# Stick-breaking attention: sums over later key blocks taken on VectorE ahead of the product with ones

## The chip, the cores and the metric

The kernel runs on one core of one Trainium2 chip. The metric is the device time of one execution in microseconds. TensorE (PE) multiplies matrices, VectorE (DVE), ScalarE (ACT) and GpSimd (POOL) work on tiles, SyncE (SP) issues most DMAs. Tiles lie in SBUF, products in PSUM, which has eight banks of 128 x 512 numbers.

## The reference

Two layers of a streaming encoder over 512 frames with 1024 features. Each layer has a token mixer with three groups of heads (retention, stick-breaking attention, gated linear attention), which share one input projection and one output projection, and then a feed-forward part with a short convolution. What the change touches is the stick-breaking group, six heads a layer:

```python
def stick_breaking(q, k, v):
    for blk in range(s // SB_BLOCK):            # blocks of 128 queries
        z = einsum('bhtd,bhsd->bhts', q[block], k[:end]) * d ** -0.5
        strict = s_idx < t_idx
        log_keep = where(strict, log_sigmoid(-z), 0.0)
        between = cumsum(log_keep, reverse=True) - log_keep
        a = where(strict, exp(log_sigmoid(z) + between), 0.0)
        outs.append(einsum('bhts,bhse->bhte', a, v[:end]))
```

For a query t and a key s, the weight is the sigmoid of z(t,s) times the product of 1 - sigmoid over all keys between s and t. In logarithms that is a sum over the later keys.

## The kernel before

The scores are held with keys on the partitions and queries along the columns. Key block i (128 keys) meets the queries from block i on, so it is 512 - 128 i columns wide. `REG` gives the place of each block: block 0 in PSUM tile 0 (512 columns), block 1 in tile 1 (columns 0 to 383), block 2 in tile 2 (256 columns), block 3 in tile 1 (columns 384 to 511). A "part" below is one of these PSUM tiles.

With L = softplus(z) (masked), the exponent that is wanted is z minus the sum of L over the same and later keys up to the query. `sb_head` makes it in three steps. First the scores and the mask go into the three PSUM tiles. Then, part by part in the order 2, 1, 0, ScalarE takes |z|, exp and ln (L780, and twice the helper at L226), VectorE adds max(z, 0) (L783), and the result L is split in two halves of the fast matmul format: ScalarE casts the high half (L785), VectorE subtracts it from L for the low half (L786). Last, TensorE adds -L to the scores: for block i the product of a triangle of -1 (`tri`) with block i's own L, and one product of a matrix of -1 (`negones`) with the L of each later block, each for the high and the low half: ten pairs, 20 products. Then ScalarE takes the exponential of each part, and `weigh` multiplies with the values.

The mixer is written as generators that are pumped in the order of a string of tokens: g for the linear attention, s for stick-breaking and retention in turn, p for a step of the input projection, f for a step of the conditioning vectors (VectorE reductions over `ada` tiles, L255). The program's scheduler then orders each engine's instructions from this; each engine takes its own in that order. So projection products (tiles `pj`) stand between the products of a head. All matmuls are issued at the recorder's line L92. Tiles of 128 x 512 (`T`, names `m__...`) share one pool of 52 buffers, and the scores of all chains share five PSUM banks (`ps`). Weights come by DMA as `raw`, and are split into `hi` (L361, ScalarE) and `lo` (L362, VectorE).

Of the kernel before, what the change touches and what calls it, by code (L numbers as in the profile page):

```python
# [12 lines left out]
F32R = mybir.dt.float32r  # L13
# [3 lines left out]
ALU = mybir.AluOpType  # L17
AX = mybir.AxisListType

P = 128  # L20
# [78 lines left out]
def trunk(ctx: ExitStack, tc: tile.TileContext, A, out, dbg=None):  # L99
# [18 lines left out]
    def nm(s):  # L118
        cnt[0] += 1
        return f"{s}_{cnt[0]}"  # L120

    def T(tag="m", shape=(P, 512), dt=F32):
        tag = TMAP.get(tag, tag)
        return tiles[tag].tile(list(shape), dt, tag=tag, name=nm(tag + "_"))
# [11 lines left out]
    def psz():  # L136
        return bank("pz")
# [7 lines left out]
    V, SC, G, PE = nc.vector, nc.scalar, nc.gpsimd, Recorder(nc.tensor)  # L145

    @contextmanager
    def seq(kind):

        mode = MODE[kind]  # L150
        m = (None, PE.last, PE.lastp)[mode]
        if m is not None:
            with tc.issue_after(m.ins):
                yield
        else:
            yield
        if kind == "p":
            PE.lastp = PE.last

    lastw = [None]  # L160
    start = {"on": True, "ld": None, "pe": None, "ws": []}
# [21 lines left out]
    def as32(t):  # L183
        return t.bitcast(F32)
# [39 lines left out]
    def act(*a, **k):  # L224
        with tc.issue_after(tables[0].ins):
            last_act[0] = SC.activation(*a, **k)  # L226
# [150 lines left out]
    REG = ((0, 0, 512), (1, 0, 384), (2, 0, 256), (1, 384, 128))  # L377
# [24 lines left out]
    def scores(par, qs, ql, ks):  # L402
        ps = [psz() for _ in range(3)]
        for i, (b, o, w) in enumerate(REG):
            kc, qc = slice(i * P, i * P + P), slice(i * P, S)
            PE.matmul(ps[b][:, o : o + w], ks[par][:, kc], qs[par][:, qc], start=(i < 3), stop=False, skip_group_check=True)
            PE.matmul(ps[b][:, o : o + w], ks[par][:, kc], ql[par][:, qc], start=False, stop=True, skip_group_check=True)
        return ps
# [38 lines left out]
    C = {}  # L447
# [95 lines left out]
    def mixer(l, hnh, hnl, after):  # L543
# [225 lines left out]
        def sb_head(par, qs, ql, ks, at):  # L769
            with seq("s"):  # L770
                ps = scores(par, qs, ql, ks)
                for i, (b, o, w) in enumerate(REG):
                    PE.matmul(ps[b][:, o : o + P], C["identb"], C["negm"], start=False, stop=True,
                              skip_group_check=True)
            Lh, Ll = [None] * 3, [None] * 3
            for b in (2, 1, 0):
                w = WID[b]
                z = ps[b][:, :w]
                e = T()
                SC.activation(e[:, :w], z, AF.Abs)  # L780
                act(e[:, :w], e[:, :w], AF.Exp, scale=-1.0)
                act(e[:, :w], e[:, :w], AF.Ln, bias=onec, scale=1.0)
                V.scalar_tensor_tensor(e[:, :w], z, 0.0, e[:, :w], ALU.max, ALU.add)  # L783
                Lh[b], Ll[b] = T("hl", dt=F32R), T("hl", dt=F32R)
                SC.copy(Lh[b][:, :w], e[:, :w])  # L785
                V.tensor_tensor(Ll[b][:, :w], e[:, :w], as32(Lh[b][:, :w]), ALU.subtract)  # L786
                at[par][b] = e
            yield
            with seq("s"):
                for i in (3, 2, 1, 0):  # L790
                    b, o, w = REG[i]
                    for i2 in range(i, 4):
                        b2, o2, w2 = REG[i2]
                        m = C["tri"] if i2 == i else C["negones"]
                        d = (i2 - i) * P
                        for X in (Lh, Ll):
                            PE.matmul(ps[b][:, o + d : o + w], m, X[b2][:, o2 : o2 + w2], start=False, stop=True,
                                      skip_group_check=True)
            for b in (2, 1, 0):
                act(at[par][b][:, : WID[b]], ps[b][:, : WID[b]], AF.Exp)  # L800
            yield

        def sb_pair(j):
            (qs, ql), ks = need(f"sq{j}", f"sk{j}")
            at = [[None] * 3, [None] * 3]
            for par in range(2):
                yield from sb_head(par, qs, ql, ks, at)
            need("sv")
            with seq("s"):
                o = weigh(at, sv, P * j)  # L810
            mh[3 + j], ml[3 + j] = split(o)
            tap(f"sb{l}{j}", as32(mh[3 + j]))
            yield
# [76 lines left out]
        for tb in range(NTB):  # L890
            cs = slice(tb * P, tb * P + P)
            ps = psz()
# [76 lines left out]
    if WARM:  # L969

        ps = psz()
# [21 lines left out]
    b2 = pv[0][:, PV["sh1"] : PV["sh1"] + 2 * KT].rearrange("p (n k) -> p n k", n=2)  # L993
# [174 lines left out]
```

## Time and profile before

| | us |
|---|---|
| median of 3 runs (1389.92 to 1395.08) | 1392.14 |
| the profiled execution | 1393.45 |
| its span, first to last instruction | 1391.7 |
| TensorE busy | 1354.5 (97%) |
| VectorE busy | 838.3 (60%) |
| ScalarE busy | 633.3 (46%) |
| GpSimd busy | 54.0 (4%) |

The profile is one execution. An engine's busy time is the union of its instructions. Matmuls overlap and their ends are modelled, so the distance from one start to the next says what a matmul costs in a row of them. The heads of layer 0 lie between 95 and 275 us, those of layer 1 between 780 and 980 us.

### The profile page before, as it was taken

The numbers are of one execution on the slowest core, as the hardware profiler recorded it, in microseconds if no ns is written. First come the engines' busy times: TensorE is split into PE (matmuls) and PEld (weight loads), VectorE is DVE, ScalarE is ACT, GpSimd is POOL, SyncE is SP. The second block draws the span as 40 slices with busy tenths as digits, with TensorE's granted clock in tenths as the row PEclk, the third lists the DMA queues.
The fourth block names the chain that finished last, engine by engine and source line by source line (L and its number), as shares of the span: only waits on it lengthen the run. The fifth ranks groups of instructions, "written<-read, shape, count | busy, mean of one in ns | idle before, by whom it ended". The sixth has DMA issues, their size and how long they took to land.

```text
span 1391.7 us, 19758 instructions
## 1 busy us (share of the span) xinstructions
PE 1354.5 (97%) x7619; PEld 1110.6 (80%) x7619; DVE 838.3 (60%) x1572; ACT 633.3 (46%) x1033; POOL 54.0 (4%) x97
## 2 busy tenths in 40 slices
PE   8999999999999999999999999999999999999997
PEld 5887667767988888888899877777898888888886
DVE  4559988665888874424563587776565444443232
ACT  5455465765543333322254556675564333332220
POOL 1000000001000000000020000000010000000000
PEclk9999999999999999999999999999999999999999
DMA  9635461204677852233753222111343223222233
GB/s 323 222 119 170 156 210 59 77 32 165 233 254 254 260 187 100 91 105 119 241 172 123 69 92 76 46 62 61 122 151 113 99 92 106 91 98 100 91 106 106
DMA packets 73999, 186.22 MB, mean 134 GB/s; under 512 B 8833, under 2 KB 9905, under 8 KB 73905
## 3 DMA queue, kind: packets, MB, share of 16 engines
q1 hardware_dynamic: 72512, 182.68, 38.9%
q0 software_dynamic: 1088, 2.12, 0.4%
q8 instruction: 60, 0.98, 0.3%
q14 instruction: 35, 0.28, 0.1%
q10 hardware_dynamic: 304, 0.16, 0.1%
HBM read 176.51 MB, written 8.41 MB: 133 GB/s over the span
## 4 chain that ended last, share of the span: by engine, by line
PE 65%; DVE 5%; ACT 3%; DMA 1%; issue 1%; POOL 0%; DVEq 0%; POOLq 0%; SPq 0%; ACTq 0%
PE pj L92 40%; PE ps L92 25%; DVE lo L362 1%; ACT hi L361 1%; DMA m__707_3526<-x 0%; DMA m__1755_9280<-x 0%; DMA raw<-wu 0%; DMA raw<-wT 0%; ACT junk L516 0%; ACT junk L307 0%; POOL s L295 0%; DVE hnl L342 0%; ACT m__1632_8684 L226 0%; DVE m__1675_8921 L742 0%; DVE m__1460_7779 L742 0%
## 5 line engine op out<-in xcount | busy, mean ns | idle before, releaser
L362 DVE TENSOR_TENSOR lo<-raw,hi 128x1024 fp32r<-128x1024 f32 (+2 forms) x208 | 245.7, 1183 | 258.2 <-ACT hi L361 250.0
L92 PE MATMUL pj<-hnh,lo 128*128 128x512 f32 x976 | 382.3, 392 | 2.0 <-DVE lo L362 2.0
L92 PE MATMUL pj<-hnh,hi 128*128 128x512 f32 x976 | 383.6, 393 | 0.0
L92 PE MATMUL pj<-hnl,hi 128*128 128x512 f32 x976 | 382.1, 392 | 0.0
L361 ACT CAST hi<-raw 128x1024 fp32r<-128x1024 f32 (+2 forms) x208 | 211.5, 1018 | 334.9 <-PE pj L92 171.0
L92 PEld LDWEIGHTS pj<-hnh,lo 128*128 128x128 f32 x976 | 183.7, 188 | 40.5 <-DVE lo L362 2.3
L92 PEld LDWEIGHTS pj<-hnh,hi 128*128 128x128 f32 x976 | 183.7, 188 | 39.7 <-issue 2.8
L92 PEld LDWEIGHTS pj<-hnl,hi 128*128 128x128 f32 x976 | 183.6, 188 | 37.7 <-issue 0.8
L255 DVE SCALAR_TENSOR_TENSOR ada<-ada,cB 128x512 f32<-128x512 f32 x160 | 107.2, 686 | 32.1 <-DMA ada<-ada 31.1
L92 PE MATMUL pj<-hi,hnh 128*128 128x384 f32 (+1 forms) x160 | 51.2, 320 | 0.0
L92 PE MATMUL pj<-lo,hnh 128*128 128x384 f32 (+1 forms) x160 | 50.9, 318 | 0.0
L92 PE MATMUL pj<-hi,hnl 128*128 128x384 f32 (+1 forms) x160 | 50.9, 318 | 0.0
L295 POOL TENSOR_TENSOR s<-s,nhalf 128x1 f32<-128x1 f32 x32 | 20.4, 638 | 760.0 <-DVE s L293 756.4
L92 PE MATMUL ps<-hnl,hi 128*128 128x256 f32 x128 | 36.4, 288 | 1.1 <-DVE hnl L342 1.1
L92 PE MATMUL ps<-hnh,lo 128*128 128x256 f32 x128 | 35.8, 284 | 0.0
L92 PE MATMUL ps<-hnh,hi 128*128 128x256 f32 x128 | 35.8, 289 | 0.0
L524 ACT ACTIVATE junk<-ps 128x512 bf16<-128x512 f32 x16 | 9.6, 597 | 51.5 <-PE ps L92 51.3
L92 PEld LDWEIGHTS pj<-hi,hnh 128*128 128x128 f32 x160 | 30.1, 188 | 0.5
L92 PEld LDWEIGHTS pj<-lo,hnh 128*128 128x128 f32 x160 | 30.0, 188 | 0.3
L92 PEld LDWEIGHTS pj<-hi,hnl 128*128 128x128 f32 x160 | 30.1, 188 | 0.0
L92 PEld LDWEIGHTS ps<-hnl,hi 128*128 128x128 f32 x128 | 24.6, 193 | 1.5 <-DVE hnl L342 1.3
L92 PEld LDWEIGHTS ps<-hnh,hi 128*128 128x128 f32 x128 | 24.7, 197 | 0.0
(2786 smaller groups left out, 2485.5 us busy)
## 6 DMA issues: line engine op xcount, KB each, us to landing
raw<-wu SPq DMA_DIRECT2D x88, 512.0 KB, 3.3
ada<-ada SPq DMA_DIRECT2D x160, 256.0 KB, 3.5
raw<-wd SPq DMA_DIRECT2D x44, 512.0 KB, 3.2
raw<-wT SPq DMA_DIRECT2D x42, 512.0 KB, 3.5
raw<-wo SPq DMA_DIRECT2D x16, 512.0 KB, 3.2
raw<-wsv SPq DMA_DIRECT2D x8, 384.0 KB, 3.6
raw<-wrv SPq DMA_DIRECT2D x8, 384.0 KB, 3.1
raw<-wgv SPq DMA_DIRECT2D x8, 272.0 KB, 2.7
```

Of the source, the lines that this page charges most:

```text
L92: self.last = self.e.matmul(*a, **k)
L255: V.scalar_tensor_tensor(raw, raw, 1.0, cB[h], ALU.mult, ALU.mult, accum_out=pt[:, 4 * h + j : 4 * h + j + 1])
L295: G.tensor_tensor(r, v, nhalf, ALU.pow)
L361: SC.copy(h, raw)
L362: V.tensor_tensor(l_, raw, as32(h), ALU.subtract)
L524: SC.activation(junk, ps, AF.Square, accum_out=ss)
```

## The change

VectorE forms the sums of L over the later blocks, and each block has one product with `negones` for each half instead of one for each later block. Part 1 comes first now. The unused half of part 2's tile takes L2 (a copy on GpSimd) and L2 + L3 for the queries that have both, so that it holds what block 1 needs; a further tile s takes L1 (a copy on GpSimd) and L1 + L2 (+ L3), which block 0 needs. Both are split into halves as L is.

```diff
-            Lh, Ll = [None] * 3, [None] * 3
-            for b in (2, 1, 0):
+            Lh, Ll, E_ = [None] * 4, [None] * 4, [None] * 3
+            for b in (1, 2, 0):
                 w = WID[b]
                 z = ps[b][:, :w]
                 e = T()
...
                 V.scalar_tensor_tensor(e[:, :w], z, 0.0, e[:, :w], ALU.max, ALU.add)
+                E_[b] = at[par][b] = e
+                if b == 2:
+                    G.tensor_copy(e[:, 256:384], e[:, 0:128])
+                    V.tensor_tensor(e[:, 384:512], e[:, 128:256], E_[1][:, 384:512], ALU.add)
+                    w = 512
                 Lh[b], Ll[b] = T("hl", dt=F32R), T("hl", dt=F32R)
                 SC.copy(Lh[b][:, :w], e[:, :w])
                 V.tensor_tensor(Ll[b][:, :w], e[:, :w], as32(Lh[b][:, :w]), ALU.subtract)
-                at[par][b] = e
+                if b == 2:
+                    s = T("hl")
+                    G.tensor_copy(s[:, 0:128], E_[1][:, 0:128])
+                    V.tensor_tensor(s[:, 128:384], E_[1][:, 128:384], e[:, 256:512], ALU.add)
+                    Lh[3], Ll[3] = T("hl", dt=F32R), T("hl", dt=F32R)
+                    SC.copy(Lh[3][:, :384], s[:, :384])
+                    V.tensor_tensor(Ll[3][:, :384], s[:, :384], as32(Lh[3][:, :384]), ALU.subtract)
             yield
             with seq("s"):
                 for i in (3, 2, 1, 0):
                     b, o, w = REG[i]
-                    for i2 in range(i, 4):
-                        b2, o2, w2 = REG[i2]
-                        m = C["tri"] if i2 == i else C["negones"]
-                        d = (i2 - i) * P
-                        for X in (Lh, Ll):
-                            PE.matmul(ps[b][:, o + d : o + w], m, X[b2][:, o2 : o2 + w2], start=False, stop=True,
-                                      skip_group_check=True)
+                    for X in (Lh, Ll):
+                        PE.matmul(ps[b][:, o : o + w], C["tri"], X[b][:, o : o + w], start=False, stop=True,
+                                  skip_group_check=True)
+                    for X in (Lh, Ll) if i < 3 else ():
+                        t, c = ((X[3], 0), (X[2], 256), (X[1], 384))[i]
+                        PE.matmul(ps[b][:, o + P : o + w], C["negones"], t[:, c : c + w - P], start=False, stop=True,
+                                  skip_group_check=True)
```

In the changed file the new lines stand as follows: L787 and L795 are the copies on GpSimd, L788 and L796 the additions on VectorE, L791 and L792 the halves of a part (before L785 and L786), L798 and L799 the halves of s; Abs is L781 (before L780).

ScalarE's order in the first head, from the cast of the second part on. ps_189, ps_188 and ps_187 are parts 2, 1 and 0; an exponential that reads a ps tile into an m tile without onec is the final one. Before:

```order
L785 CAST m__194_1025<-m__193_1020 128x512
L780 ACTIVATE m__196_1029<-ps_187_996 128x512
L226 ACTIVATE m__196_1029<-m__196_1029 128x512
L226 ACTIVATE m__196_1029<-m__196_1029,onec_99 128x512
L226 ACTIVATE m__190_1011<-ps_189_998 128x256
L226 ACTIVATE m__193_1020<-ps_188_997 128x512
L785 CAST m__197_1034<-m__196_1029 128x512
```

With the change:

```order
L791 CAST m__194_1027<-m__193_1020 128x512
L798 CAST m__197_1034<-m__196_1031 128x384
L226 ACTIVATE m__193_1020<-ps_189_998 128x256
L226 ACTIVATE m__190_1011<-ps_188_997 128x512
L781 ACTIVATE m__199_1038<-ps_187_996 128x512
L226 ACTIVATE m__199_1038<-m__199_1038 128x512
L226 ACTIVATE m__199_1038<-m__199_1038,onec_99 128x512
L791 CAST m__200_1043<-m__199_1038 128x512
```

The final exponentials of parts 2 and 1 stood behind part 0's Abs, Exp and Ln, and stand ahead of them now; the cast of s (L798) has come in ahead of both. Over the twelve heads, both stand ahead of part 0's Abs in five, that of part 2 alone in four, none in three.

TensorE's order at the products into part 0 of the first head (ps_187), from the product with the low half's triangle on. Before:

```order
L92 MATMUL ps_187_996<-m__198_1035,tri_642 128x512
L92 MATMUL ps_187_996<-m__194_1025,negones_646 128x384
L92 MATMUL ps_187_996<-m__195_1026,negones_646 128x384
L92 MATMUL ps_187_996<-m__191_1016,negones_646 128x256
L92 MATMUL ps_187_996<-m__192_1017,negones_646 128x256
L92 MATMUL ps_187_996<-m__194_1025,negones_646 128x128
L92 MATMUL ps_187_996<-m__195_1026,negones_646 128x128
L92 MATMUL pj_241_1256<-lo_201_1041,hnh_3_116 128x384
```

With the change:

```order
L92 MATMUL pj_244_1259<-hi_212_1067,hnl_4_117 128x384
L92 MATMUL ps_187_996<-m__200_1043,tri_642 128x512
L92 MATMUL ps_187_996<-m__201_1044,tri_642 128x512
L92 MATMUL ps_187_996<-m__197_1034,negones_646 128x384
L92 MATMUL ps_187_996<-m__198_1035,negones_646 128x384
L92 MATMUL pj_267_1356<-hi_203_1049,hnh_3_116 128x384
```

The six products with negones are two, both over the sum tile s, and the two with the triangle stand next to each other without projection products between.

## Rows read from the trace of the kernel before

**Rows 1.** The page's head and first block: span; busy us, share, instructions.

```profile
span 1391.7 us, 19758 instructions
...
PE 1354.5 (97%) x7619; PEld 1110.6 (80%) x7619; DVE 838.3 (60%) x1572; ACT 633.3 (46%) x1033; POOL 54.0 (4%) x97
```

**Rows 2.** Stretches: length, busy PE, PEld, DVE, ACT, POOL, clock, DMA.

```profile
95.00:275.00 180.00, 170.04 (x1255) 131.22 (x1254) 153.66 (x339) 106.78 (x181) 10.24 (x19) 0.99 0.42 138
...
340.00:705.00 365.00, 361.00 (x1704) 302.87 (x1703) 234.59 (x475) 130.23 (x188) 12.62 (x22) 1.00 0.56 185
...
780.00:980.00 200.00, 193.91 (x1444) 150.93 (x1443) 146.70 (x271) 127.85 (x217) 7.51 (x13) 1.00 0.18 61
```

**Rows 3.** Timeline of TensorE, head one, block 1: start, duration, instruction.

```profile
104.19 0.22 PE L92 MATMUL ps<-m__194_1025,negones 128*128 128x128 f32 x1
...
104.36 0.39 PE L92 MATMUL pj<-hi,hnl 128*128 128x384 f32 x1
```

**Rows 4.** Timeline of TensorE, head one, block 0; idle time in brackets.

```profile
107.19 0.50 PE L92 MATMUL ps<-m__198_1035,tri 128*128 128x512 f32 x1 [0.19 <-DVE m__198_1035 L786]
...
107.88 0.28 PE L92 MATMUL ps<-m__191_1016,negones 128*128 128x256 f32 x1
...
108.12 0.22 PE L92 MATMUL ps<-m__194_1025,negones 128*128 128x128 f32 x1
...
108.29 0.39 PE L92 MATMUL pj<-lo,hnh 128*128 128x384 f32 x1
```

**Rows 5.** Timeline of ScalarE, head one.

```profile
96.09 0.39 ACT L780 ACTIVATE m__190_1011<-ps 128x256 f32<-128x256 f32 x1 [1.16 <-PE ps L92]
...
98.46 0.41 ACT L785 CAST m__191_1016<-m__190_1011 128x256 fp32r<-128x256 f32 x1 [1.00 <-DVE m__190_1011 L783]
98.77 0.59 ACT L780 ACTIVATE m__193_1020<-ps 128x512 f32<-128x512 f32 x1
...
101.55 0.62 ACT L785 CAST m__194_1025<-m__193_1020 128x512 fp32r<-128x512 f32 x1 [0.76 <-DVE m__193_1020 L783]
102.07 0.59 ACT L780 ACTIVATE m__196_1029<-ps 128x512 f32<-128x512 f32 x1
...
103.99 0.37 ACT L226 ACTIVATE m__190_1011<-ps 128x256 f32<-128x256 f32 x1
...
105.14 0.62 ACT L785 CAST m__197_1034<-m__196_1029 128x512 fp32r<-128x512 f32 x1
```

**Rows 6.** Timeline of VectorE, head one, two low halves.

```profile
99.03 0.42 DVE L786 TENSOR_TENSOR m__192_1017<-m__190_1011,m__191_1016 128x256 fp32r<-128x256 f32 x1
...
102.52 0.69 DVE L786 TENSOR_TENSOR m__195_1026<-m__193_1020,m__194_1025 128x512 fp32r<-128x512 f32 x1
```

**Rows 7.** Timeline of VectorE, a retention pair, other widths.

```profile
239.79 0.55 DVE L827 TENSOR_TENSOR m__488_2466<-ps,m__346_1789 128x384 f32<-128x384 f32 x1
...
240.59 0.28 DVE L827 TENSOR_TENSOR m__488_2466<-ps,m__346_1789 128x128 f32<-128x128 f32 x1
```

**Rows 8.** Timeline of GpSimd, 345 to 348 us.

```profile
345.45 0.55 POOL L295 TENSOR_TENSOR s<-s,nhalf 128x1 f32<-128x1 f32 x1 [5.40 <-DVE s L293]
347.32 1.57 POOL L295 TENSOR_TENSOR s<-s,nhalf 128x1 f32<-128x1 f32 x1 [1.31 <-DVE s L293]
```

**Rows 9.** Timeline of VectorE at the same time.

```profile
347.25 1.23 DVE L362 TENSOR_TENSOR lo<-raw,hi 128x1024 fp32r<-128x1024 f32 x1
```

**Rows 10.** Groups of GpSimd: busy us, mean ns of one, idle before.

```profile
L664 POOL TENSOR_TENSOR m__178_950<-m__178_950,m__179_951 128x512 f32<-128x512 f32 x1 | 1.3, 1294 | 57.4 <-ACT m__178_950 L226 57.4
...
L247 POOL MEMSET mod1g<- 128x24 f32 x2 | 0.3, 138 | 0.0
```

**Rows 11.** Timeline of TensorE, after a wait at 167 us.

```profile
169.24 0.50 PE L92 MATMUL pj<-hnh,lo 128*128 128x512 f32 x1 [2.01 <-DVE lo L362]
...
170.62 0.63 PE L92 MATMUL pj<-hnh,hi 128*128 128x512 f32 x1
171.04 0.63 PE L92 MATMUL pj<-hnl,hi 128*128 128x512 f32 x1
```

## The prediction

> **What bounds the kernel now.** I read the page's first block, then the kernel cut into stretches, then, for the stretches that the change touches, the timelines of TensorE, ScalarE and VectorE around one head, and last what TensorE waited for. The first block says TensorE: busy for 1354.5 of 1391.7 us, with VectorE at 60% and ScalarE at 46% [rows 1]. The stretches say where that holds [rows 2]. In a feed-forward part (340 to 705 us) TensorE is busy for 361.00 of 365 us. The twelve stick-breaking heads lie in 95 to 275 us (layer 0) and 780 to 980 us (layer 1). There TensorE is idle for 180 - 170.04 = 9.96 us and 200 - 193.91 = 6.09 us, together 16.05 us, while VectorE is busy 85% and 73% of the time. So TensorE bounds the heads' stretches too, but not alone: part of the time it waits for a chain that runs over ScalarE and VectorE. Within a head the reader is to see products with tri and negones that stand between projection products (pj), which fill TensorE while a head's chain runs, and a wait where the chain comes late: 0.19 us ahead of the second product of part 0 in head one [rows 4].
>
> **What is removed.** Per head the list of products with L falls from 20 to 14. Gone are, each twice (high and low half): block 3 into block 1 (128 columns), block 2 into block 0 (256) and block 3 into block 0 (128). Matmuls overlap, so a matmul's price is not its 0.22 to 0.28 us but the distance to the next start. In head one the pair into block 1 takes 104.36 - 104.19 = 0.17 us [rows 3]; the pairs into block 0 take 108.12 - 107.88 = 0.24 us and 108.29 - 108.12 = 0.17 us [rows 4]. That is 0.58 us a head and 12 x 0.58 = 7.0 us in all. The products that stay keep their widths and prices.
>
> **What is added.** On VectorE, per head: an addition over 128 columns (0.28 us, as the 128-column row of the retention scores), one over 256 columns (0.42 us), the low half of part 2 over 512 instead of 256 columns (0.69 - 0.42 = 0.27 us) and the low half of the new sum over 384 columns (0.55 us) [rows 6, 7]. Together 1.52 us, 18.2 us in twelve heads. On ScalarE: the cast of part 2 over 512 instead of 256 columns (0.62 - 0.41 = 0.21 us) and a cast over 384 (between these two, 0.52 us) [rows 5], 0.73 us a head, 8.8 us in all. Both engines have room for it (153.66 and 146.70 us busy become some 163 and 156 of 180 and 200), so these microseconds cost nothing where projection products cover them; where that cover is gone they are waits of TensorE.
>
> On GpSimd: two copies of 128 x 128 a head, which the trace of before does not show. The nearest rows bound one between 0.14 us (a memset of 24 columns) and 1.29 us (a sum of two inputs over 512 columns) [rows 10]; by columns the second makes 0.32 us, and I take 0.35 us. Each copy runs beside the VectorE addition for the same tile (0.28 and 0.42 us), so at that price it adds under 0.1 us to a head.
>
> **What is moved.** This is where the gain can go. ScalarE's queue in head one now runs 9.67 us from the first Abs (96.09) to the end of part 0's cast (105.14 + 0.62) [rows 5]. In the new order I add up the same rows: part 1 first, 102.07 - 98.77 = 3.30; part 2, 98.77 - 96.09 = 2.68, plus the addition ahead of its cast 0.28 and the wider cast 0.21, 3.17; then the cast of the new sum waits for part 2's low half and the addition on VectorE, 0.69 + 0.42 = 1.11, and takes 0.52. In head one both final exponentials now stand ahead of part 0's Abs (order shown with the change); they took 105.14 - 103.99 = 1.15 us, which used to lie in the wait for VectorE's L783. Part 0 follows: 103.99 - 102.07 = 1.92, the wait for VectorE that part 1 shows, 0.76, and the cast 0.62. Sum 12.55 us, 2.88 us more. In five of the twelve heads the order has both exponentials ahead, in four only the short one (0.37 us, so 2.10 more), in three none (1.73 more): (5 x 2.88 + 4 x 2.10 + 3 x 1.73) / 12 = 2.33 us a head in the mean, a chain 24% longer.
>
> How much of that TensorE feels, no row shows. From below it is nothing, since projections fill; even some of the 16.05 us could go, since a part's products now wait for fewer tiles. From above it is all of 12 x 2.33 = 28.0 us. I take the value nearest to what the trace shows for the chain as it is: the 16.05 us of idle time grow by the same 24%, 3.9 us. (Some of these waits belong to other chains, which makes it high; the missing slack makes it low.)
>
> **Sum.** The profiled execution took 1393.45 us, 1391.7 of span and 1.75 around it, 1.3 us above the median of the three runs, 1392.14. Against it: -7.0 + 3.9 = -3.1 us, 1390.3; against the median 1389.0. I predict 1389 us.
>
> **Rivals.**
>
> *The whole gain arrives.* Projections cover all of the longer chain, and a fifth of the idle time (3 us) goes because part 1 starts a head and its products wait for fewer halves: 1392.1 - 7.0 - 3.0 = 1382 us. For it speaks that TensorE is busy 94% and 97% of the heads' stretches, so there is work to fill with; against it that VectorE at 85% answers late.
>
> *Slower: part 0's chain is exposed.* Mechanism: ScalarE stands at the cast of the new sum, which waits for VectorE, and behind it in the same queue stand part 0's Abs, Exp and Ln, and behind these TensorE's widest products. If two thirds of the 2.33 us a head are exposed, 18.7 - 7.0 = +11.7 us, 1404 us. It decides from 0.58 us a head on (25% of the lengthening) for slower at all, from 1.17 us on for slower by 0.5%. For it: the wait of rows 4 sits at this very product. A long wait costs twice: after 2.01 us of waiting for a weight tile, TensorE's rows are spaced 171.04 - 170.62 = 0.42 us [rows 11], where the feed-forward part takes 361.00 / 1704 = 0.21 us for one in the mean [rows 2]: the lower of the two clock levels (1.2 GHz for 2.4) for a while. Against: products of other chains stand between.
>
> *The copies meet VectorE.* GpSimd's one-column power takes 0.55 us [rows 8], but 1.57 us where a VectorE subtraction of two SBUF tiles began 0.07 us earlier and ended 0.41 us before it [rows 8, 9]. If the copies lose half of that 1.02 us each, the head's chain grows by another 1.0 us to 3.3 (34%), the idle time by 5.5 us: 1390.6; if VectorE is the one held up, 24 x 0.35 = 8.4 us of the busier engine come on top, at worst in full, 1399. I put this rival at 1394 us. The Trainium skill ("SBUF — State Buffer", section "Who interferes with whom") states the rule: a VectorE instruction with two SBUF inputs contends with a GpSimd instruction that reads SBUF, not with one that only writes it. By that rule the two rows are the expected picture; GpSimd's many memsets here would be harmless, and the new copies, which read, would not.
>
> *Nothing moves.* The removed products stood where TensorE would have waited anyway, and the chain's growth is covered: 1392 us. The change itself does what it says; the order shows four products into block 0 where eight stood.
>
> **How the numbers follow.** Chances: forecast 0.43 (1389, its own range 1385 to 1396), whole gain 0.25 (1382), exposed chain 0.19 (1404), copies 0.08 (1394), nothing 0.05 (1392). What a measurement of this kernel can tell from no change is about 0.5%, 7 us: 1385 and 1399. Faster beyond that: the whole gain and a twelfth of the forecast, 0.29. Slower: the exposed chain and half of the copies, 0.23. Same: 0.48. The range leaves out a tenth at each end: 1379 to 1404.
>
> **What would show it.** Right: 72 matmuls fewer; VectorE up by about 18 us and ScalarE by about 9 us; TensorE's idle time in the heads' stretches at about 20 us; these stretches together some 3 us shorter, the feed-forward parts unchanged. The first rival shows idle time under 14 us, the exposed chain over 25 us with waits for L791, L792, L798 or L799, the copies GpSimd rows far above 0.35 us at L787 and L795. Wrong altogether would be a difference outside the heads' stretches.

## The result, and the profile after

The changed kernel takes 1425.99 us in the median (1424.88 to 1428.66) where the kernel before took 1392.31 beside it: a ratio of 1.0231 [1.0206, 1.0255]. It is 37 us above the forecast, and above the range. The page's head says how the 32.7 us between the two profiled spans divide.

```profile
span 1424.4 us, 19718 instructions
...
PE 1362.8 (96%) x7547; PEld 1107.5 (78%) x7547; DVE 855.1 (60%) x1608; ACT 638.9 (45%) x1045; POOL 62.4 (4%) x121
```

Against [rows 1]: the 72 matmuls are gone, VectorE has 16.8 us more and ScalarE 5.6, GpSimd 8.4 for its 24 copies. So the change does what it says. TensorE's idle time grew from 37.2 to 61.6 us (24.4 us), and its busy time grew by 8.3 us although it has less to do. Where, the stretches show (columns as in [rows 2]):

```profile
95.00:275.00 180.00, 161.80 (x1142) 121.26 (x1141) 151.26 (x338) 99.51 (x168) 12.53 (x25) 0.94 0.40 128
275.00:340.00 65.00, 54.60 (x311) 40.64 (x310) 38.81 (x70) 37.12 (x64) 2.69 (x6) 0.89 0.17 57
340.00:705.00 365.00, 360.22 (x1708) 302.63 (x1707) 232.19 (x464) 134.75 (x199) 10.50 (x18) 1.00 0.55 183
780.00:980.00 200.00, 191.52 (x1306) 146.04 (x1306) 142.31 (x251) 121.09 (x206) 11.74 (x25) 0.97 0.22 72
```

The feed-forward part is as before. The heads of layer 0 start where they did, but TensorE does 1142 matmuls in 180 us where it did 1255, idle for 18.2 us instead of 9.96, at a granted clock of 0.94. In the 65 us behind, where the last head of layer 0 now ends (291.4 us instead of 272.8), it is idle for 10.4 us where it was idle for 2.82. In layer 1 the heads end at 976.9 us instead of 942.5, and part of what they lose falls behind 980 us. The 65 us of before:

```profile
275.00:340.00 65.00, 62.18 (x330) 48.44 (x329) 38.04 (x77) 35.86 (x68) 2.87 (x6) 0.97 0.23 82
```

Finer stretches show where the clock falls; first three of the kernel after, then the same of before:

```profile
200.00:220.00 20.00, 14.52 (x53) 8.56 (x52) 14.49 (x28) 11.18 (x20) 2.02 (x4) 0.74 0.50 159
280.00:300.00 20.00, 10.56 (x66) 7.32 (x58) 13.08 (x22) 12.01 (x22) 2.69 (x6) 0.79 0.23 79
900.00:920.00 20.00, 15.18 (x82) 8.01 (x81) 11.61 (x19) 13.89 (x25) 2.33 (x3) 0.74 0.09 27
```

```profile
200.00:220.00 20.00, 19.57 (x92) 13.45 (x93) 15.48 (x28) 13.74 (x24) 0.00 (x0) 1.00 0.46 148
280.00:300.00 20.00, 18.46 (x130) 12.60 (x130) 11.69 (x29) 8.62 (x16) 0.00 (x0) 0.91 0.08 27
900.00:920.00 20.00, 20.00 (x158) 15.15 (x157) 18.51 (x35) 11.57 (x20) 0.00 (x0) 1.00 0.23 80
```

The longest waits of TensorE between 95 and 300 us (line and tile waited for; total, times, longest) are for the casts of the heads (L791), and one at the end of layer 0's mixer for the linear attention; the last line is the longest of layer 1, between 780 and 990 us:

```profile
PE ps L95 <- DVE m__587_2916 L709: 6.2, 1, 6.2
PE ps L92 <- ACT m__265_1352 L791: 4.0, 1, 4.0
PE ps L92 <- ACT m__380_1886 L791: 2.5, 1, 2.5
PE ps L92 <- ACT m__566_2806 L791: 2.2, 1, 2.2
PE ps L92 <- ACT m__406_2022 L791: 2.0, 1, 2.0
...
PE ps L92 <- ACT m__1535_8041 L791: 4.8, 1, 4.8
```

Added up over the whole trace, TensorE waited 2.7 us for casts of the heads in the kernel before (six waits) and 21.0 us in the changed one (15 waits). That is 18.3 of the 24.4 us of new idle time.

The second line is head two. TensorE there (start, duration, instruction, idle time and its releaser in brackets):

```profile
130.66 0.40 PE L92 MATMUL pj<-hnh,lo 128*128 128x512 f32 x1
130.99 0.69 PE L92 MATMUL ps<-m__243_1254,m__242_1253 64*64 64x64 f32 x32
132.75 1.07 PE L92 MATMUL ps<-m__199_1038,m__122_664 128*64 128x512 f32 x2 [1.07 <-ACT m__258_1329 L226]
137.79 0.76 PE L92 MATMUL ps<-m__265_1352,tri 128*128 128x512 f32 x1 [3.97 <-ACT m__265_1352 L791]
138.52 0.80 PE L92 MATMUL ps<-m__266_1353,tri 128*128 128x512 f32 x1
...
139.75 0.63 PE L92 MATMUL pj<-hnh,hi 128*128 128x512 f32 x1
140.18 0.63 PE L92 MATMUL pj<-hnl,hi 128*128 128x512 f32 x1
...
144.34 0.40 PE L92 MATMUL pj<-hnh,hi 128*128 128x512 f32 x1
144.57 0.40 PE L92 MATMUL pj<-hnl,hi 128*128 128x512 f32 x1
```

One projection product stands ahead of the gap, then 3.97 us in which TensorE stands before part 0's product; the next projection products are behind it in the queue, and none waits for anything when its turn comes. After the wait equal products start 0.43 us apart, and 0.23 us from 144.34 on: the lower of the two levels (1.2 GHz) and then the upper (2.4). The granted clock of the trace is 1.00 from 120 to 131 us, 0.72 from 137.8 to 144 and 1.00 from 144.3 to 146. What kept part 0 is in ScalarE's timeline:

```profile
128.01 0.62 ACT L791 CAST m__259_1336<-m__258_1329 128x512 fp32r<-128x512 f32 x1 [0.76 <-DVE m__258_1329 L788]
130.95 1.05 ACT L361 CAST hi<-raw 128x1024 fp32r<-128x1024 f32 x1 [2.32 <-DMA raw<-wT]
131.90 0.51 ACT L798 CAST m__262_1343<-m__261_1340 128x384 fp32r<-128x384 f32 x1
132.32 0.38 ACT L226 ACTIVATE m__258_1329<-ps 128x256 f32<-128x256 f32 x1
132.59 0.59 ACT L226 ACTIVATE m__255_1320<-ps 128x512 f32<-128x512 f32 x1
133.07 0.60 ACT L781 ACTIVATE m__264_1347<-ps 128x512 f32<-128x512 f32 x1
...
136.17 1.04 ACT L361 CAST hi<-raw 128x1024 fp32r<-128x1024 f32 x1 [1.09 <-DMA raw<-wT]
137.12 0.61 ACT L791 CAST m__265_1352<-m__264_1347 128x512 fp32r<-128x512 f32 x1
```

Part 2's cast ends at 128.63, part 0's Abs starts at 133.07. Between them stand the cast of the sum, both exponentials and a weight cast that waits 2.32 us for its DMA. A second weight cast, which waits 1.09 us, stands ahead of part 0's own cast. In the kernel before part 0's cast was through by then; its weight cast came behind it:

```profile
128.61 0.62 ACT L785 CAST m__259_1340<-m__258_1335 128x512 fp32r<-128x512 f32 x1 [0.52 <-DVE m__258_1335 L783]
131.15 1.05 ACT L361 CAST hi<-raw 128x1024 fp32r<-128x1024 f32 x1 [1.91 <-DMA raw<-wT]
```

One number sums this up, and it is used below: the *chain* of a head, from the start of its first Abs to the end of part 0's last low half (of the sum's, where that comes later). In head one it ran from 96.09 [rows 5] to 107.14 (VectorE's low half began at 106.46 and took 0.68), 11.05 us; after, from 95.77 to 109.86:

```profile
95.77 0.60 ACT L781 ACTIVATE m__190_1011<-ps 128x512 f32<-128x512 f32 x1 [1.20 <-PE ps L92]
```

```profile
109.17 0.69 DVE L792 TENSOR_TENSOR m__201_1044<-m__199_1038,m__200_1043 128x512 fp32r<-128x512 f32 x1
```

Taken so from the timelines, the mean of the twelve heads is 12.69 us before and 15.53 us after, 2.84 us more a head, 34.1 us in all.

### The profile page after: what moved, and what is told of

Read it like the earlier page. It is cut to its first block, busy times and chain, and to the rows that moved or that the text cites. A ratio compares the mean times of both kernels' runs of the same rounds, so it can differ in the third digit from the quotient of the medians.

```text
span 1424.4 us, 19718 instructions
## 1 busy us (share of the span) xinstructions
PE 1362.8 (96%) x7547; PEld 1107.5 (78%) x7547; DVE 855.1 (60%) x1608; ACT 638.9 (45%) x1045; POOL 62.4 (4%) x121
## 4 chain that ended last, share of the span: by engine, by line
PE 71%; DVE 12%; DMA 9%; ACT 5%; issue 2%; POOL 0%; SPq 0%; DVEq 0%; POOLq 0%; ACTq 0%
PE pj L92 39%; PE ps L92 32%; DMA ada<-ada 6%; DVE lo L362 3%; DVE ada L255 2%; ACT hi L361 1%; DMA raw<-wT 1%; DMA m__1820_9429<-x 0%; DMA m__117_557<-ada 0%; DVE hnl L342 0%; DMA m__725_3544<-x 0%; DMA m__7_122<-x 0%; DMA m__1247_6554<-x 0%; DMA m__1836_9506<-x 0%; DVE m__180_958 L701 0%
## 5 line engine op out<-in xcount | busy, mean ns | idle before, releaser
L255 DVE SCALAR_TENSOR_TENSOR ada<-ada,cB 128x512 f32<-128x512 f32 x160 | 106.9, 687 | 30.8 <-DMA ada<-ada 30.1
```

The source lines that it names most:

```text
L255: V.scalar_tensor_tensor(raw, raw, 1.0, cB[h], ALU.mult, ALU.mult, accum_out=pt[:, 4 * h + j : 4 * h + j + 1])
```

## The experiments

Ratios are to the kernel before, run beside each on the same chip, with 95% intervals. A chain is the mean of the twelve heads in one execution, the profiled one; a ratio comes from several executions.

### First: order, place, copies, products

**e1_order.** The kernel before, parts in the order of the change.

```diff
-            for b in (2, 1, 0):
+            for b in (1, 2, 0):
```

> The kernel before, with only the order of the parts changed from (2, 1, 0) to (1, 2, 0); no sums, the 20 products a head as before. Theory Q (ScalarE's queue: part 0's Abs stands behind the cast of the new sum, which waits for VectorE): the order alone is harmless, 1387 to 1398 us. Theory O (the order of the parts itself: with the wide part first, the final exponentials and the first products come late): most of the 34 us loss is already here, 1410 us or more. Theory C (the GpSimd copies are slow or hold up VectorE) and theory D (the added VectorE and ScalarE work lengthens the chain of a head wherever it stands): 1387 to 1398 us, as Q.

Ratio 1.000 [0.998, 1.002], chain 12.74 us. Theory O falls.

**e2_late_sum.** The block `if b == 2: s = ...` of the changed kernel, moved behind the loop over parts.

> The changed kernel, with the new sum for block 0 (copy, addition, cast, low half) made after part 0's Abs, Exp, Ln and halves instead of ahead of them; the same instructions, in another order. Theory Q: part 0 no longer waits behind the sum, at least two thirds of the 34 us come back: 1390 to 1404 us. Theory D: the same work still has to end before block 0's last products, so nothing comes back: 1420 to 1432 us. Theories O and C: 1420 to 1432 us.

Ratio 1.0263 [1.0233, 1.0293], chain 15.3 us. Theory Q falls in the form in which it was put: part 0 no longer stands behind the sum, but then the sum ends last, and the chain is as long.

**e3_copies_dve.**

```diff
-                    G.tensor_copy(e[:, 256:384], e[:, 0:128])
+                    V.tensor_copy(e[:, 256:384], e[:, 0:128])
...
-                    G.tensor_copy(s[:, 0:128], E_[1][:, 0:128])
+                    V.tensor_copy(s[:, 0:128], E_[1][:, 0:128])
```

> The changed kernel, with the two copies of 128 x 128 a head on VectorE instead of GpSimd. Theory C: without GpSimd on the path and beside VectorE, at least half of the loss comes back: 1396 to 1410 us. Theories Q, O and D: VectorE has 24 short copies more, some 0.2 us each on a busy engine, 1424 to 1434 us.

Ratio 1.0275 [1.0244, 1.0306], chain 15.86 us. Theory C falls.

**e4_sums_old_products.** The changed kernel with the loop over `i2` of the kernel before in place of the new products.

> The changed kernel with all its sums, copies, casts and order, but the 20 products a head of the kernel before (the new sums are made and not used). It separates what the added work costs from what the missing products save. If the removed products were on the path (7.0 us by their distances): 1430 to 1436 us. If TensorE would stand waiting in their place anyway: 1422 to 1429 us, as the changed kernel. If theory Q needs the products to wait for the sum itself, rather than for part 0 behind it: below 1410 us.

Ratio 1.0257 [1.0238, 1.0277], chain 16.23 us. 3.6 us more than the changed kernel, within the two intervals: the loss comes with the sums, and the missing products save little. In microseconds (1432.48) this is the first of the expected ranges, but the kernel before took 1397.54 beside it, 5 us more than with the result.

### Second: load against length

**e5_dve_load, e6_act_load.** The kernel before, with work behind the loop over parts that nothing waits for; one on VectorE, one on ScalarE.

```diff
+            V.tensor_reduce(scr[:, 0:1], at[par][1], mybir.AxisListType.X, ALU.add)
+            V.tensor_reduce(scr[:, 1:2], at[par][0], mybir.AxisListType.X, ALU.add)
```

```diff
+            SC.copy(junk[:, :256], at[par][0][:, :256])
+            SC.copy(junk[:, :128], at[par][1][:, :128])
```

> The kernel before, with two reductions over 512 columns a head added on VectorE behind part 0's low half, some 1.4 us a head, that nothing waits for: VectorE's load of the change without its longer chain. Theory V (VectorE is 96% busy between 100 and 140 us, so added work there delays all that stands behind it in its queue, above all the low halves of the weights at L362 that free the weight buffers; projections then come late and TensorE lacks them as fill): at least half of the loss appears, 1409 us or more. Theory L (the chain of the head itself got longer than the projections placed beside it can cover): nothing waits for these, 1391 to 1401 us. Theory B (three more tiles a head turn the ring of 52 buffers faster, so buffers come free late): 1391 to 1401 us.

> The kernel before, with two casts of 256 and 128 columns a head added on ScalarE behind part 0's cast, some 0.7 us a head, that nothing waits for: ScalarE's load of the change without its longer chain. Theory V: ScalarE has room, 1391 to 1400 us. Theory L: 1391 to 1400 us. At 1405 us or more ScalarE's queue would be the one that hands its delay on.

Ratios 1.0050 [1.0033, 1.0066] and 1.0015 [0.9997, 1.0033], chains 12.44 and 12.65 us. VectorE's load by itself costs 7 us, a fifth of the loss: theory V has a part, not the most.

**e7_adds_pool.** Both `V.tensor_tensor(..., ALU.add)` of the sums on GpSimd.

> The changed kernel, with the two additions a head on GpSimd as well as the copies: VectorE loses 0.28 + 0.42 = 0.70 of the 1.5 us that were added a head, and the chain of a head gets longer, since GpSimd takes 1.29 us for a sum of two inputs over 512 columns. Theory V: a third to a half of the loss comes back, 1408 to 1416 us. Theory L: slower still, 1428 us or more. Theory B: 1424 to 1432 us.

Ratio 1.0229 [1.0205, 1.0253], 1425.80 us, chain 15.0 us. Of the three ranges only that of theory B has this, and the next run speaks against B. The kernel is neither better for VectorE's sake, as V had it, nor worse for GpSimd's, as L had it; the longer chain that L counted on did not come.

**e8_nm47.** `NM` 52 to 47 in the kernel before.

> The kernel before, with 47 buffers in the ring instead of 52 (three tiles more a head on some 28 use the ring up about 10% faster). Theory B: most of the loss appears, 1410 us or more. Theories V and L: the ring has slack, 1391 to 1400 us.

Ratio 1.0035 [1.0016, 1.0054], chain 12.66 us. Five buffers are worth 5 us here, not 34: theory B falls as the main cause.

### Third: the length itself

**e9_hops.** The kernel before, with a step on GpSimd in each part.

```diff
                 V.scalar_tensor_tensor(e[:, :w], z, 0.0, e[:, :w], ALU.max, ALU.add)
+                G.tensor_copy(e[:, :256], e[:, :256])
```

> The kernel before, with one GpSimd copy of 256 columns onto itself in each of the three parts of a head, between VectorE's L783 and ScalarE's cast: no work added on TensorE, VectorE or ScalarE, only a longer chain, some 0.5 to 0.6 us a hop. Theory L in figures: from a head's first Abs to the end of its last low half the traces show 12.69 us in the mean before and 15.53 us after; 12 x 2.84 = 34.1 us is the whole loss, so every microsecond of the chain is exposed. It expects 12 x 1.6 = 19 us, 1406 to 1422 us. Theory V (VectorE's load) and theory C (GpSimd beside VectorE) expect 1391 to 1400 us.

Ratio 1.0064 [1.0042, 1.0086], chain 14.10 us. The chain grew by 1.41 us; 12 x 1.41 = 16.9 us of chain made 9 us of time, between the ranges of theories L and V. A longer chain costs. How much of it is not settled here: the chain is that of the slowest of seven executions (1408.73 us), 15.3 us above the profiled one of before, and against the median it is about half.

**e10_after_no_ln.** The changed kernel without the third step of each part.

```diff
-                act(e[:, :w], e[:, :w], AF.Ln, bias=onec, scale=1.0)
```

> The changed kernel without the logarithm of the three parts (left out: ScalarE's L783, so the sums are not those of the reference): about 1.95 us less on ScalarE a head, nothing less on VectorE, GpSimd and TensorE. Theory L: 12 x 2.0 = 24 us come back, 1396 to 1408 us. Theory V: VectorE is as busy as ever, 1418 to 1428 us.

Ratio 1.0038 [1.0017, 1.0060], chain 13.16 us. All additions, copies and wider halves are still there, and 1.9 of the 2.3% are gone: 27 us for 12 x 2.37 = 28.4 us of chain. Theory V would have had nothing come back.

**e11_pipe_after.** The changed kernel in another order of issue: `front` is Abs, Exp, Ln and VectorE's L784, `halves` the cast and the low half.

```diff
+            e1 = front(1)
+            e2 = front(2)
+            halves(1, e1, 512)
+            G.tensor_copy(e2[:, 256:384], e2[:, 0:128])
+            V.tensor_tensor(e2[:, 384:512], e2[:, 128:256], e1[:, 384:512], ALU.add)
+            s = T("hl")
+            G.tensor_copy(s[:, 0:128], e1[:, 0:128])
+            V.tensor_tensor(s[:, 128:384], e1[:, 128:384], e2[:, 256:512], ALU.add)
+            e0 = front(0)
+            halves(2, e2, 512)
+            halves(3, s, 384)
+            halves(0, e0, 512)
```

> The changed kernel with ScalarE's steps of a head shifted against each other: the Abs, Exp and Ln of the next part are issued ahead of the cast of the part before, and the casts of part 2, of the sum and of part 0 come last. The same instructions, but ScalarE no longer stands at a cast that waits for VectorE or GpSimd. By the rows of the trace its queue then needs 1.95 + 1.31 + 0.62 + 1.95 + 0.62 + 0.52 + 0.62 = 7.6 us a head. Theory L: the chain gets shorter than before's and the removed products show, 1375 to 1394 us. If instead the products that now come late together leave TensorE without work (a rival: what counts is when the first products are ready): 1405 us or more. Theory V: 1418 us or more.

Ratio 0.9930 [0.9908, 0.9953], 1385.79 us, chain 10.25 us. The page shows the same counts on TensorE, VectorE, ScalarE and GpSimd as the changed kernel, and a span 38.3 us shorter:

```profile
span 1386.1 us, 19715 instructions
...
PE 1348.4 (97%) x7547; PEld 1105.6 (80%) x7547; DVE 853.6 (62%) x1608; ACT 632.8 (46%) x1045; POOL 67.5 (5%) x121
```

In head two ScalarE takes the next Abs, Exp and Ln ahead of casts at which it stood before. At the first cast it still stands for 1.76 us; part 0's cast comes at 129.67 instead of 137.12:

```profile
123.82 0.62 ACT L790 CAST m__257_1330<-m__255_1320 128x512 fp32r<-128x512 f32 x1 [1.76 <-DVE m__255_1320 L785]
124.34 0.59 ACT L782 ACTIVATE m__260_1339<-ps 128x512 f32<-128x512 f32 x1
124.97 0.63 ACT L226 ACTIVATE m__260_1339<-m__260_1339 128x512 f32<-128x512 f32 x1
125.86 0.62 ACT L790 CAST m__261_1344<-m__256_1325 128x512 fp32r<-128x512 f32 x1 [0.26 <-DVE m__256_1325 L797]
...
129.67 0.62 ACT L790 CAST m__265_1352<-m__260_1339 128x512 fp32r<-128x512 f32 x1
```

Over the whole trace TensorE now waits 0.6 us for casts of the heads, where it waited 21.0.

**e12_pipe_before.** The same shift in the kernel before: front(2), front(1), halves(2), front(0), halves(1), halves(0).

> The kernel before with the same shift of ScalarE's steps, order of the parts (2, 1, 0), no sums, 20 products a head: the control for the run above. Theory L if the kernel before is bound by the chain too: 1372 to 1388 us. If its chain is just covered by projections (a knee at 12.7 us, so that longer costs and shorter brings nothing): 1388 to 1397 us.

Ratio 0.9905 [0.9874, 0.9935], 1382.60 us, chain 9.46 us. It is faster than the kernel before and than the changed one. The chain limited the kernel before as well. Against e11, with 14 products in a chain 0.8 us longer, the intervals overlap.

```profile
span 1377.7 us, 19761 instructions
...
PE 1347.1 (98%) x7619; PEld 1108.5 (80%) x7619; DVE 838.5 (61%) x1572; ACT 627.9 (46%) x1033; POOL 54.1 (4%) x97
```

### Fourth: what is left of the saving

**e14_pipe_sum_pool.** e12 and a sum for block 0 only, after halves(2); block 0 then has one product with `negones` for each half, 16 products a head:

```diff
+            s = T("hl")
+            G.tensor_copy(s[:, 0:128], e1[:, 0:128])
+            G.tensor_tensor(s[:, 128:384], e1[:, 128:384], e2[:, 0:256], ALU.add)
+            G.tensor_tensor(s[:, 256:384], s[:, 256:384], e1[:, 384:512], ALU.add)
```

> The shifted kernel with 20 products (the control, ratio 0.9905) plus only the sum for block 0, made wholly on GpSimd (a copy and two additions) beside part 0's Abs, Exp and Ln; part 2 stays 256 columns wide, 16 products a head, two wide pairs replaced. By the rows 12 x (0.24 + 0.17) = 4.9 us of products go; ScalarE gets one cast (0.52 us) and VectorE one low half (0.55 us) a head. If the saving shows once the chain no longer grows: 1374 to 1381 us where the control has 1382.6. If a microsecond of chain still costs what it did around the kernel before (some 4 us for 12 heads) and products are covered: 1383 to 1389 us.

Ratio 0.9952 [0.9935, 0.9970], chain 10.13 us: the products saved don't pay for 0.67 us of chain.

**e15_pipe_after_pool.** e11 with the two additions on GpSimd.

> The shifted changed kernel (ratio 0.993, chain 10.25 us) with its two additions a head on GpSimd too. If VectorE's queue is what keeps its chain 0.8 us longer than the control's: 1378 to 1385 us. If GpSimd's slower additions stand on the path: 1388 us or more.

Ratio 0.9980 [0.9966, 0.9995], chain 10.82 us: GpSimd's slower additions stand on the path.

**e16_pipe_old_products.** e11 with the old loop over `i2`.

> The shifted changed kernel with all its sums, and the 20 products a head of the kernel before: the same chain, so the difference to the run with 14 products is what six products a head are worth when the chain is short. If they are worth their distances, 7.0 us: 1390 to 1396 us. If projections only move up into their place or TensorE waits there instead: 1384 to 1388 us.

Ratio 0.9961 [0.9945, 0.9977], chain 10.07 us. Its 1390.57 us lie at the edge of the first range. Against e11 that is 0.3% for six products a head, with intervals that overlap: not settled, hence the last two.

**e17_pipe_hops.** e12 with two GpSimd copies of 256 columns onto themselves in `halves`.

> The control (shifted, 20 products, chain 9.46 us) with two GpSimd copies of 256 columns in each part between VectorE's L784 and the cast. In the shifted order the next part's Abs, Exp and Ln lie beside them, so only part 0's two stay on the path, some 1.0 to 1.5 us a head. If time follows the length of the chain: chain 10.5 to 11 us, 1385 to 1391 us. If the hops cost by themselves (GpSimd beside VectorE, six a head where three cost 9 us): 1398 us or more.

Ratio 1.0033 [1.0014, 1.0053], chain 11.39 us. Its 1399.74 us lie in the range of the second theory, that the hops cost by themselves, and the ratio is slower than the chain would have it: at 12.69 us the kernel before is at 1.000. But the chain is that of the fastest of ten executions, 1392.86 us or 0.998 of the kernel before, and there it fits its place. The other nine show a granted clock of 0.988 to 0.994 where this one shows 0.998; what their chains were, no trace here shows.

**e18_before_left_out, e19_pipe_left_out.** The kernel before, and e12, without the three pairs that the change removes.

```diff
-                    for i2 in range(i, 4):
+                    for i2 in range(i, min(i + 2, 4)):
```

> The kernel before with the three pairs of products a head that the change removes left out, and nothing added (the L of blocks 2 and 3 are then missing in block 0, and that of block 3 in block 1): 14 products, order and chain as before. It measures the first term of the sum by itself. Worth their distances: 7.0 us, ratio 0.995. If TensorE waits for the chain in their place, or projections would have stood there: 0.998 to 1.000.

> The same three pairs left out of the shifted kernel, whose chain is 3.2 us a head shorter: the same term where TensorE waits less. Worth their distances: 7.0 us less than the shifted kernel with 20 products, ratio 0.9855 where that has 0.9905. If the products are hidden there too: 0.989 to 0.992.

Ratios 1.0014 [0.9995, 1.0032] and 0.9876 [0.9853, 0.9898]. At the chain of the kernel before the products are worth nothing; with the short chain some 4 us (0.9876 against 0.9905), which overlapping intervals do not make certain. The page of e18 shows where the saving went: TensorE is busy 3.9 us less than in [rows 1], and idle for 46.5 us instead of 37.2. (This execution is 5.5 us longer than the profiled one of before, where the ratio says 2.0, so some of that is the spread between executions.)

```profile
span 1397.1 us, 19619 instructions
...
PE 1350.6 (97%) x7547; PEld 1105.4 (79%) x7547; DVE 837.7 (60%) x1572; ACT 632.9 (45%) x1033; POOL 53.1 (4%) x97
```

## Why the prediction was wrong

Twelve of the kernels in the order of their chains (mean us a head; the others are in the sections above):

| run | products | chain | ratio |
|---|---|---|---|
| e12, shifted | 20 | 9.46 | 0.9905 |
| e16, shifted, sums not used | 20 | 10.07 | 0.9961 |
| e14, shifted, one sum | 16 | 10.13 | 0.9952 |
| e11, shifted, the change | 14 | 10.25 | 0.9930 |
| e15, the same, additions on GpSimd | 14 | 10.82 | 0.9980 |
| e17, shifted, hops | 20 | 11.39 | 1.0033 |
| before | 20 | 12.69 | 1 |
| e10, the change without Ln | 14 | 13.16 | 1.0038 |
| e9, hops | 20 | 14.10 | 1.0064 |
| e7, additions on GpSimd | 14 | 15.0 | 1.0229 |
| after | 14 | 15.53 | 1.0231 |
| e4, sums, old products | 20 | 16.23 | 1.0257 |

**The step that failed: the exposure of the longer chain, taken at 3.9 us.** The prediction scaled the idle time of TensorE (16.05 us) by the growth of the chain. But idle time is what is left where the fill ran out; it says nothing of how near the fill is to running out elsewhere. What came is near the bound from above (28.0 us, with the growth as measured 12 x 2.84 = 34.1 us): 32.7 us between the spans. Of these, 24.4 us are idle time, and about 12 us the lower clock: e18 does the same 7547 matmuls in 1350.6 us of busy time, the changed kernel in 1362.8. The granted clocks of the two traces bear that out: TensorE's busy time, multiplied stretch by stretch with the share of the clock that was not granted, comes to 7.6 us in e18 and 19.6 in the changed kernel. The 3.9 us that e18 is busy less than before go the other way: 24.4 + 12.2 - 3.9 = 32.7. That loss and lengthening come out so close is in part chance: 18.3 us are waits for the heads' casts, and the rest is the lower clock and waits for other things.

The price is not a straight line. From 9.46 to 12.69 us twelve heads pay 13 of 39 us of chain, a third; from 13.16 to 15.53 nearly all (27 of 28.4). Between these stands e9 alone, whose share is open. The table is not one curve: e5 lost 0.5% by load alone; e2 (15.30 us, 1.0263) and e3 (15.86, 1.0275) stand out of order, though within the intervals; and e17's chain is that of its fastest execution.

What the chains grew by can be read from ScalarE's timelines. Within the twelve chains ScalarE stands ahead of the heads' casts for 18.3 us before, 43.8 after and 11.2 in e11. Weight casts and the waits ahead of them take 26.1, 33.4 and 13.7 us, a term that the prediction did not have; the heads' casts themselves grew by 8.7 us, and the other pieces shrank by 7.4. So three quarters of the 34.1 us is standing at casts. But the length counts, whatever fills it: in e10 ScalarE still stands for 40.6 us, and 27 us came back with the logarithm of each part left out.

**The term of -7.0 us failed too.** Distances between starts were read rightly, but a removed product saves its distance only where TensorE is what is waited for. e18 gives +2.0 us [-0.7, +4.5] for it. The work did go: with the part that was not granted by the clock taken out, as above, TensorE's busy time is 1349.4 us before and 1343.0 in e18, 6.4 us less. The 9.3 us of new idle time and 2.5 us of lower clock took it up. The reading behind the term, "TensorE bounds the heads' stretches too, but not alone", at 94 and 97% busy, was the root of both errors: e12 has every product of the kernel before and a span 14.0 us shorter, because its heads end sooner. The Trainium skill ("Perfetto Trace Analysis", section "Identifying the Most-Contended Engine") says that the busy share of matmuls is no good measure of how close TensorE is to its peak, and has its headroom judged by the arithmetic done and by the busy share of weight loads. [Rows 2] agree: weight loads take 131.22 of 180 us (73%) and 150.93 of 200 us (75%) in the heads' stretches, 302.87 of 365 us (83%) in the feed-forward part. That was a sign that the heads had room, and it was not used.

**Right, or nearly.** The growth of the chain, 2.33 us, measured 2.84. VectorE's 18.2 us and ScalarE's 8.8 us: the durations of the instructions concerned grew by 18.6 and 8.7, the engines' busy time by 16.8 and 5.6. The 72 matmuls. The signs named for the exposed chain: idle time over 25 us in the heads' stretches (18.20 + 8.48 = 26.7), with waits for L791. Projections in the heads were said to be the cover; they are, and TensorE stood where those placed ahead of a head's product ran out.

**The rivals.** "Part 0's chain is exposed" had the mechanism, the releasers (L791, L792 and the low clock after a wait) and the sign, at two thirds of the chain and with 7.0 us taken off: 1404. With the whole of 2.84 us and nothing taken off it is 1393.45 + 34.1 = 1427.6 us. Its place was too narrow: not the cast of the sum alone (e2; 12.3 of the 43.8 us are spent ahead of it), but the whole chain, with every cast at which ScalarE stands while another engine answers. e11 takes most of that standing away, with the same instructions, and is 38.3 us shorter. "The copies meet VectorE" falls: 24 copies took 8.4 us, 0.35 us each as taken, and e3 without them is no faster. Single copies took up to 0.75 us (at 102.56, beside a VectorE instruction on two tiles at L255). The Trainium skill's rule ("SBUF — State Buffer", section "Who interferes with whom") would have that; it decides nothing here. "The whole gain" and "nothing" fall with the verdict.

**What stays open.** The traces divide the length of the chain, but not the time lost, between the standing at casts and the weight casts that now fall into the chain (2.32 and 1.09 us of waiting in head two); e11 moves both. The scheduler's placing of projections differs from kernel to kernel and was not held fixed, so that e11 and e12 act through the chain alone is argued from TensorE's waits for the casts (21.0 us after, 0.6 in e11), not shown. Each chain is from one execution.

## What to carry to other kernels

Where several engines work on one piece in turn, ask of an edit first what it does to the length of that chain, and price the growth from its upper bound where the filling engine already waits at the chain's products. Before trusting a saving on an engine that is 95% busy, leave the work out and time that. Look for instructions that stand in an in-order queue for another engine's answer: shifting them by one part (e12) gained 13 us, while removing 72 products from the same kernel (e18) gained none.

## What the runs showed of the hardware

An idle TensorE costs twice: after 3.97 us of waiting its products started 0.43 us apart, and 0.23 us only some 6 us later. In three stretches of 20 us the granted clock was 0.74, 0.79 and 0.74, where the kernel before shows 0.91 at the lowest. With five of 52 tile buffers taken away the kernel was 0.35% slower, and with 1.4 us a head of VectorE work that nothing waits for 0.5%.
